# First attention values: a weight's cast ahead of the tile of h, its low parts behind the scaled tile, the next tile's modulation last

## The chip, the cores and the metric

One core of a Trainium2 chip runs the whole kernel in one launch. The metric is device time in microseconds; lower is better. Times are medians of several runs; the profile comes from one profiled execution, whose own time is given beside its span. The engines are TensorE (PE in the profile; PEld is its weight load), VectorE (DVE), ScalarE (ACT), GpSimd (POOL) and SyncE (SP), which issues nearly all transfers.

## The reference

One decoder block on x (1024 tokens by 1024 features) with a conditioning vector c. What matters here is its start:

```python
mod = silu(c) @ w_ada + b_ada
sh1, sc1, g1, sh2, sc2, g2 = split(mod, 6)
h = rms_norm(x, norm1_g) * (1 + sc1) + sh1
proj = h @ w_in        # retention q, k, v, gate; attention q, k, v for 3 groups of heads; 2 gates
```

Then come retention, dilated window attention in three groups, a gated merge with an output projection, a second normalised and modulated h with a squared-ReLU MLP, and a last RMS normalisation. Everything is float32.

## The kernel before, in words

**Number format.** TensorE multiplies fp32r operands. Each float32 operand is split into a high part (a cast to fp32r, on ScalarE) and a low part (the rest, a subtraction on VectorE). A product is the sum of three matmuls: low weight with high x, high weight with low x, high with high.

**Layout of the start.** h is kept transposed, as 8 tiles of 128 features by 1024 tokens: `hh[k]` high, `hl[k]` low. The normalisation's row factor is one row `rb1`, copied to all 128 partitions. The shift and the scale of tile k are columns `SH1 + k` and `SC1 + k` of `mods`, each the row sums of a 128x1024 tile of `w_ada` (`early`, shown as `em`) times a tile that holds silu(c) in every partition (`cb`). One such product with its sum is one VectorE instruction and a read of the accumulator.

**What is done for one tile** (helpers at lines 428 to 462):

- `mod1(k, parts)` (L433): the two products with row sums for scale and shift, from `early` tiles that SyncE loads in the start.
- `h1_mods(k)` (L448, L449): two instructions on 128x1 columns: add the bias to the shift, make the factor `a1`.
- `h1_scale(k)` (L456, L458): VectorE scales the tile `xt[k]` by `a1` and `rb1`, then ScalarE adds the shift and casts: `hh[k]`.
- `h1_low(k)` (L461): VectorE: `xt[k]` + shift - `hh[k]`, the low part `hl[k]`. It needs `hh[k]`.

**First attention values** (`av_first`, L768; `av_k`, L735). The values of attention group g are h @ w_av[g], 8 blocks of 128 tokens by 512 columns, one PSUM bank each, all 8 banks in use. For each k there are 24 matmuls of 128x512: from k = 1 on first 16 with `hh[k]` (low and high weight in turn), then 8 with `hl[k]`. For group 0 the tiles of h are made while they are used: the body of step k makes the tile k + 1 and the modulation of k + 2, and then issues the matmuls of k. One weight tile of 128x1024 covers two k's, so `ahead(1)` in every even k prepares the next step's weight. The start-up (`startup`, L371) has prepared the first weight, tile 0 of h and the modulation of tile 1.

**Weights.** `split_w` (L180) does both parts at once: the cast on ScalarE (L183), the subtraction on VectorE (L184). `split_first` (L759) does the cast alone (L762) and puts the subtraction (L763) on the list `first["lows"]`, to be called later; before, only the very first weight uses it.

**What sets the order.** There is no scheduler: each engine runs its instructions in the order in which the program emits them, and waits on semaphores for the others. `Steps` (L55) walks through a list of steps with their loads; three raw weight buffers (`raw`) are in turn, and the weight parts have three buffers each. `prepare` casts a loaded tile and then issues the load that takes the next buffer in turn; that transfer, on SyncE's queue (L85), waits until the old contents are read, which is after the subtraction. `first["release"]()` at k = 3 lets the loads beyond the first three be issued; SyncE itself runs ahead as far as its waits let it. The order of SyncE's queue in the stage is: the `em` and `xt` tiles with three weights between, four more weights, the attention bias tables (`bias_out`, L421), the next weight, the stores of the values.

**Behind it** the attention values of groups 1 and 2 follow (`av_step`, L832), then queries, keys and gates.

Of the kernel before, what the change touches and what calls it, by code (L numbers as in the profile page):

```python
# [20 lines left out]
NK = D // P  # L21
# [111 lines left out]
def block_kernel(ctx, tc, io, stop=None, dbg=None):  # L133
# [3 lines left out]
    def fv(t):  # L137
        return t.bitcast(F32)
# [36 lines left out]
    SH1, SC1, G1, SH2, SC2, G2 = (8 * i for i in range(6))  # L175

    steps = Steps(nc, wraw, 3)
# [187 lines left out]
    first = {"lows": []}  # L365
# [55 lines left out]
    def bias_out(g):  # L421

        nc.sync.dma_start(brow_d[g], bias_cut(rows, g)[:12])
        for a in range(4):
            src = brow_d[g][4 * g + a:4 * g + a + 1]
            nc.sync.dma_start(bias_d[g][a], src.to_broadcast([P, 384]))

    def mod1(k, parts=(SC1, SH1)):

        for i in parts:  # L430
            i += k
            t = early[i]
            nc.vector.scalar_tensor_tensor(t, t, 1.0, cb, op0=ALU.mult, op1=ALU.mult, accum_out=mods[:, i:i + 1])  # L433
# [12 lines left out]
    def h1_mods(k):  # L446
        sh = mods[:, SH1 + k:SH1 + k + 1]
        nc.vector.tensor_add(sh, sh, vec[:, VC_BADA + SH1 + k:VC_BADA + SH1 + k + 1])  # L448
        nc.vector.scalar_tensor_tensor(a1[:, k:k + 1], mods[:, SC1 + k:SC1 + k + 1], bs1[:, k:k + 1],  # L449
                                       vec[:, VC_N1 + k:VC_N1 + k + 1], op0=ALU.add, op1=ALU.mult)  # L450

    def h1_scale(k, j=None):

        ts = slice(0, S) if j is None else slice(512 * j, 512 * j + 512)
        t = xt[k][:, ts]
        nc.vector.scalar_tensor_tensor(t, t, a1[:, k:k + 1], rb1 if j is None else first["rb"][j],  # L456
                                       op0=ALU.mult, op1=ALU.mult)
        nc.scalar.activation(hh[k][:, ts], t, AF.Identity, bias=mods[:, SH1 + k:SH1 + k + 1])  # L458

    def h1_low(k):  # L460
        nc.vector.scalar_tensor_tensor(hl[k], xt[k], mods[:, SH1 + k:SH1 + k + 1], fv(hh[k]),  # L461
                                       op0=ALU.add, op1=ALU.subtract)
# [263 lines left out]
    def wsplit(ap):  # L726
        return ap, split_w
# [7 lines left out]
    def av_k(g, k, w):  # L735

        ws = slice((k % 2) * 512, (k % 2) * 512 + 512)
        if k == 0:
            av[g] = [ps_s(f"av{g}{c}") for c in range(NC)]
        if g == 0:  # L740

            parts = ((hh, 0), (hl, 0), (hh, 1)) if k == 0 else ((hh, 1), (hh, 0), (hl, 0))
            groups = (parts[:1], parts[1:2], parts[2:]) if k == 0 else (parts[:2], parts[2:])
        else:
            parts = ((hh, 1), (hh, 0), (hl, 0))
            groups = (parts,)
        for group in groups:
            for c in range(NC):
                for x, j in group:
                    nc.tensor.matmul(av[g][c], x[k][:, c * C:(c + 1) * C], w[j][:, ws], start=k == 0 and (x, j) == parts[0],  # L750
                                     stop=k == NK - 1 and (x, j) == parts[2], skip_group_check=True)
        for c in range(NC) if k == NK - 1 else ():
            if c % 2 == 0:
                t = x4(f"avo{g}{c}")
            o = t[:, DV * (c % 2):DV * (c % 2) + DV]
            nc.scalar.copy(o, av[g][c])
            nc.sync.dma_start(va_d[g][c * C:(c + 1) * C], o)
# [10 lines left out]
    def av_first(kk):  # L768

        def body(ahead, w):  # L770
            for k in (2 * kk, 2 * kk + 1):
                if k == 0:
                    for j, rb in enumerate(first["rb"]):
                        nc.scalar.copy(rb1[:, 512 * j:512 * j + 512], rb)
                if k + 1 < NK:
                    h1_mods(k + 1)
                    h1_scale(k + 1)
                    if k % 2 == 0:
                        ahead(1)
                    if k + 2 < NK:  # L780
                        mod1(k + 2)
                    h1_low(k + 1)
                av_k(0, k, w)
                if k == 3:
                    first["release"]()
                if k == 4:
                    for g in range(3):
                        bias_out(g)
                if k == NK - 1:
                    ahead(1)  # L790
                    nc.sync.dma_start(cs, io["cossin"])
                    nc.sync.dma_start(decay, io["decay"])
        return body
# [8 lines left out]
    def sums_of_h(name):  # L802

        low = None
        for m in range(4):
            k = 2 * m + 1
            e, o = xt[2 * m], xt[k]
            e0, e1, o0, o1 = e[:, :512], e[:, 512:], o[:, :512], o[:, 512:]
            sh = mods[:, SH1 + k:SH1 + k + 1]
            if name == "t1":  # L810
                r = e0
                nc.vector.tensor_sub(r, e0, e1)
            elif name == "t3":
                r = e1
                nc.vector.scalar_tensor_tensor(r, e1, dsh1[:, m:m + 1], o1, op0=ALU.add, op1=ALU.subtract)
            elif name == "t2":
                r = o1
                nc.vector.scalar_tensor_tensor(r, o1, sh, e0, op0=ALU.add, op1=ALU.add)
            else:
                r = o0  # L820
                nc.vector.scalar_tensor_tensor(r, o0, sh, o1, op0=ALU.add, op1=ALU.subtract)
            if name != "t4":
                t = x4(f"xa{name}{m}", F32R)
                XA[name, m] = t[:, :512], t[:, 512:]
            if low:
                nc.vector.tensor_sub(low[0], low[1], fv(low[2]))
            hi, lo = XA[name, m]
            nc.scalar.copy(hi, r)
            low = lo, r, hi
        nc.vector.tensor_sub(low[0], low[1], fv(low[2]))  # L830

    def av_step(g, kk):  # L832
        def body(w):
            if (g, kk) == (1, 0):
                for m in range(4):
                    nc.sync.dma_start(h12_d[m][:, 0], fv(hh[2 * m][:, 512:]))
                    nc.sync.dma_start(h12_d[m][:, 1], fv(hl[2 * m][:, 512:]))
                sh = mods[:, SH1:SH1 + NK].rearrange("p (m j) -> p m j", j=2)
                nc.vector.tensor_sub(dsh1, sh[:, :, 0], sh[:, :, 1])
            for k in (2 * kk, 2 * kk + 1):  # L840
                av_k(g, k, w)
            if g == 1 and kk < 3:
                sums_of_h(("t1", "t3", "t2")[kk])
            if (g, kk) == (1, 3):
                a_load(0, 1)
                a_load(0, 2)
            if (g, kk) == (2, 1):
                BA.prep((0, "11"), (0, "s1"))
            if (g, kk) == (2, 2):
                a_load(1, 1)  # L850
                a_load(1, 2)
                BA.prep((0, "s3"), (0, "s2"))
        return body
# [9 lines left out]
    def a_load(q, part):  # L863
        pair = PAIRS[q]
        src = io[{"g": "w_gate2", "a": "w_aq"}.get(pair[0]) or f"w_r{pair[1]}"]
        i = 2 * pair[1] + pair[2] if pair[0] == "a" else pair[-1]
        if q == 0 or q % 2 == 0 and part == 2:
            r = x4(f"wa{q}{part}")
        else:
            r = wraw.tile([P, 1024], F32, tag="raw", name=f"wa{q}{part}")  # L870
        nc.sync.dma_start(r, src[2 * i + part - 1])
        BA.raw[q, part] = r
# [67 lines left out]
        new_head(0)  # L940

    for kk in range(4):
        steps.add(av_first(kk), [(io["w_av"][kk], split_w if kk else split_first)], manual=True)
    for g in (1, 2):
        for kk in range(4):
            steps.add(av_step(g, kk), [wsplit(io["w_av"][4 * g + kk])])
    steps.mark()
    steps.add(queries_keys, manual=True)

# [3 lines left out]
    for h in range(H):  # L953
        steps.add(v_first(h), [wsplit(io["w_rv"][4 * h + j]) for j in range(2)], manual=True)
        steps.add(v_rest(h), [(io["w_rv"][4 * h + j], wv_prep) for j in range(2, 4)], manual=True)
        for c in range(NC):
            steps.add((lambda h, c: lambda ahead, *w: chunk(h, c, ahead, *w))(h, c),
                      ([wsplit(io["w_rg"][4 * h + c // 2])] if c % 2 == 0 else []) + [mod_load(later_mods[8 * h + c])],
                      manual=True)
# [418 lines left out]
    for pair in range(2):  # L1378
        for i, (g, a) in enumerate(combos):
# [3 lines left out]
                      manual=i == pair == 0)  # L1383
# [591 lines left out]
```

## Time and profile before

| | |
|---|---|
| median of 3 runs | 2317.35 us (2315.91 to 2317.53) |
| profiled execution, its own time | 2316.94 us |
| its span, first to last instruction | 2315.0 us |
| mean granted TensorE clock | 0.998 |
| ScalarE casts of weights in the stage | at 20.76, 31.67, 45.06, 58.46 and 71.85 us |
| first attention values: first matmul, first matmul of the next group | 23.37 us, 78.00 us |

How to read the rows. In a timeline: start in us from the span's start, duration in us, engine, source line, operation, output <- inputs with partitions x elements and type, count; in brackets the idle time before it and what ended it. In the table by stretches: start and end, length, then for each engine the busy time and the number of instructions, the granted clock of TensorE (1.00 is full), the busy share of the 16 transfer engines and GB/s. In the list of waits: who waited for whom, us in total, times, longest. An instruction's duration includes the end of its pipeline; the next one on the engine can start up to 0.1 us before that, so distances between starts are the better measure.

### The profile page before, as it was taken

Reading aid. Unit: us, or ns where it says so; the run is one execution under the profiler, and the core shown is the slowest. Engines: PE = TensorE matmul, PEld = TensorE weight load, DVE = VectorE, ACT = ScalarE, POOL = GpSimd, SP = SyncE. Lnnn points to the kernel's source line nnn. Section 1 sums busy time; section 2 is a strip of 40 time slices with the busy share of each in tenths; the row PEclk is TensorE's granted clock in tenths of the full one; section 3 lists DMA queues with packets and bytes.
Section 4 is the critical chain, followed back from the end, with each engine's and each line's share of the span. In section 5 each row is a group of like instructions: output and inputs, shape, how many; then the busy total and the mean of one; then the engine's idle time right before and its main releaser. Section 6 shows DMA issues by size and latency. Waiting matters only on the chain.

```text
span 2315.0 us, 26666 instructions
## 1 busy us (share of the span) xinstructions
PE 2261.9 (98%) x10466; PEld 1864.6 (81%) x10466; DVE 1350.1 (58%) x1986; ACT 808.2 (35%) x1479; POOL 171.7 (7%) x136
## 2 busy tenths in 40 slices
PE   6999999999999999999999999999999999999998
PEld 4787888888878787888788888888778887888887
DVE  5626555547677676855555646567855554544445
ACT  3324233222334343444535411134454444221112
POOL 0000000001101010100000014401000000000003
PEclk9999999999999999999999999999999999999999
DMA  8532333332323232233323353253223336323222
GB/s 350 192 127 99 115 114 110 110 133 104 118 86 126 89 119 91 83 130 102 96 72 96 136 174 97 90 189 118 68 108 109 109 108 218 111 91 103 98 82 73
DMA packets 101661, 274.65 MB, mean 119 GB/s; under 512 B 22423, under 2 KB 33950, under 8 KB 101407
## 3 DMA queue, kind: packets, MB, share of 16 engines
q1 hardware_dynamic: 100382, 270.85, 34.1%
q0 software_dynamic: 1152, 2.10, 0.3%
q8 instruction: 82, 1.34, 0.2%
q14 instruction: 45, 0.36, 0.1%
HBM read 208.27 MB, written 67.00 MB: 119 GB/s over the span
## 4 chain that ended last, share of the span: by engine, by line
PE 57%; DVE 5%; ACT 3%; DMA 1%; issue 1%; POOLq 0%; SPq 0%; POOL 0%; DVEq 0%; ACTq 0%
PE f L193 4%; PE f L197 4%; PE f L195 4%; PE fp L193 4%; PE fp L197 4%; PE fp L195 4%; PE ro L195 3%; PE ro L193 3%; PE ro L197 3%; PE ak L193 2%; PE ak L195 2%; PE ak L197 2%; PE rg L195 1%; PE rg L193 1%; PE wo L193 1%; PE wo L195 1%
## 5 line engine op out<-in xcount | busy, mean ns | idle before, releaser
L1768 DVE SCALAR_TENSOR_TENSOR x1r<-f,mods,x1r 128x512 f32<-128x512 f32 x112 | 78.7, 746 | 153.4 <-PE f L197 153.4
L1479 POOL TENSOR_TENSOR g<-g,rt 128x1024 f32<-128x1024 f32 x24 | 66.2, 2760 | 432.2 <-DVE rt L1478 432.2
L193 PE MATMUL qap<-hh,qaw 128*128 128x512 f32 x216 | 84.3, 390 | 3.4 <-DVE qat L277 1.7
L197 PE MATMUL qap<-hh,qaw 128*128 128x512 f32 x216 | 84.1, 389 | 0.0
L195 PE MATMUL qap<-hl,qaw 128*128 128x512 f32 x216 | 84.0, 389 | 0.0
L1478 DVE TENSOR_TENSOR rt<-ro,g 128x1024 f32<-128x1024 f32 x32 | 39.0, 1219 | 57.4 <-PE ro L197 45.2
L555 POOL TENSOR_TENSOR j<-qk,j 128x512 fp32r<-128x512 f32 x32 | 44.0, 1374 | 364.0 <-ACT j L554 364.0
L1619 ACT ACTIVATE a<-a 128x512 f32<-128x512 f32 x48 | 30.4, 633 | 110.1 <-DVE a L1618 110.1
L1521 POOL TENSOR_TENSOR accnf<-accnf,sqnf 128x256 f32<-128x256 f32 (+1 forms) x18 | 16.6, 924 | 654.5 <-ACT sqnf L1520 654.5
L250 DVE TENSOR_TENSOR qaw<-wa,qaw 128x512 fp32r<-128x512 f32 x54 | 36.7, 689 | 39.5 <-ACT qaw L240 39.5
L1109 ACT ACTIVATE P<-P,ng 128x128 f32<-128x128 f32 (+1 forms) x96 | 41.9, 438 | 40.1 <-DVE ng L1106 40.1
L250 DVE TENSOR_TENSOR fw<-w1r,fw 128x512 fp32r<-128x512 f32 x48 | 32.8, 688 | 36.2 <-ACT fw L240 36.2
L193 PE MATMUL fp<-h2h,fw 128*128 128x512 f32 x128 | 50.6, 395 | 0.5 <-ACT ft2nsq L272 0.5
L193 PEld LDWEIGHTS qap<-hh,qaw 128*128 128x128 f32 x216 | 40.5, 188 | 12.6 <-DVE qat L277 2.2
L197 PE MATMUL fp<-h2h,fw 128*128 128x512 f32 x128 | 50.3, 393 | 0.0
L195 PE MATMUL fp<-h2l,fw 128*128 128x512 f32 x128 | 50.2, 392 | 0.0
L633 ACT CAST vh<-v 128x512 fp32r<-128x512 f32 x32 | 18.8, 588 | 89.3 <-PE v L597 87.2
L575 ACT COPY sm<-sT 128x128 f32<-128x128 f32 x32 | 8.5, 267 | 113.9 <-PE sT L566 113.9
L197 PEld LDWEIGHTS qap<-hh,qaw 128*128 128x128 f32 x216 | 40.5, 188 | 8.5
L195 PEld LDWEIGHTS qap<-hl,qaw 128*128 128x128 f32 x216 | 40.5, 188 | 8.3
L240 ACT CAST qaw<-wa 128x512 fp32r<-128x512 f32 x54 | 32.5, 616 | 36.1 <-PE qap L197 36.1
L438 DVE SCALAR_TENSOR_TENSOR raw<-raw,cb 128x1024 f32<-128x1024 f32 x32 | 43.3, 1354 | 0.0
(3521 smaller groups left out, 6943.5 us busy)
## 6 DMA issues: line engine op xcount, KB each, us to landing
raw<-in_w_ada_dram SPq DMA_DIRECT2D x32, 512.0 KB, 3.5
w1r<-in_w_ff_dram SPq DMA_DIRECT2D x32, 512.0 KB, 5.2
ad<-a SPq DMA_DIRECT2D x32, 512.0 KB, 3.0
raw<-in_w_ff_dram SPq DMA_DIRECT2D x32, 512.0 KB, 3.5
raw<-ad SPq DMA_DIRECT2D x32, 512.0 KB, 4.4
em<-in_w_ada_dram SPq DMA_DIRECT2D x16, 512.0 KB, 10.2
qkd<-qa SPq DMA_DIRECT2D x16, 512.0 KB, 2.6
raw<-in_w_rv_dram SPq DMA_DIRECT2D x16, 512.0 KB, 4.4
```

The lines of the kernel that those rows point to most:

```text
L193: nc.tensor.matmul(o, wl, xh, start=first, stop=False, skip_group_check=skip)
L195: nc.tensor.matmul(o, wh, xl, start=False, stop=False, skip_group_check=skip)
L197: nc.tensor.matmul(o, wh, xh, start=False, stop=last, skip_group_check=skip)
L240: nc.scalar.copy(t[:, :512], src)
L250: nc.vector.tensor_sub(t[:, 512:], src, fv(t[:, :512]))
L438: nc.vector.scalar_tensor_tensor(raw, raw, 1.0, cb, op0=ALU.mult, op1=ALU.mult, accum_out=mods[:, i:i + 1])
L555: nc.gpsimd.tensor_sub(t[:, 1], src, fv(t[:, 0]))
L1109: nc.scalar.activation(v, v, AF.Exp, bias=ng[:, blk:blk + 1], accum_out=st[:, g, blk, 2 + a:3 + a])
L1478: nc.vector.tensor_mul(t, flat(ps), sg)
L1479: (nc.vector if h == H - 1 else nc.gpsimd).tensor_add(m, m, t)
L1619: nc.scalar.activation(o, o, AF.Relu)
L1768: nc.vector.scalar_tensor_tensor(x, ps[hf], mods[:, G2 + i:G2 + i + 1], x, op0=ALU.mult, op1=ALU.add)
```

## The change

In `av_first` three things move, and the kind of preparation of four weights changes.

- `ahead(1)`, which casts the next weight, stands at the top of an even k, in front of the tile k + 1. ScalarE thus does the cast ahead of that tile's activation.
- All weights that this stage prepares (those of steps 1 to 3 of group 0 and of step 0 of group 1) now go through `split_first`. Their subtraction is called behind the scaling of the tile k + 1, in front of its low parts.
- `h1_low(k + 1)` comes ahead of `mod1(k + 2)` where a weight was subtracted (even k), and between the scale's and the shift's part where not (odd k). Before, it came behind both.

The order of one tile's instructions on VectorE:

| | before | after |
|---|---|---|
| even k | mods, scaling, weight low, modulation x2, h low | mods, scaling, weight low, h low, modulation x2 |
| odd k | mods, scaling, modulation x2, h low | mods, scaling, modulation, h low, modulation |

and on ScalarE for an even k: before the activation, then the cast; after the cast, then the activation. The counts of instructions on all engines stay the same, and so does the order on TensorE and SyncE. For the last subtraction of the stage there is a call behind the matmuls of k = 7, which finds an empty list.

```diff
@@ -772,14 +772,23 @@
                     for j, rb in enumerate(first["rb"]):
                         nc.scalar.copy(rb1[:, 512 * j:512 * j + 512], rb)
+                if k % 2 == 0:
+                    ahead(1)
                 if k + 1 < NK:
                     h1_mods(k + 1)
                     h1_scale(k + 1)
-                    if k % 2 == 0:
-                        ahead(1)
-                    if k + 2 < NK:
-                        mod1(k + 2)
-                    h1_low(k + 1)
+
+                    if first["lows"]:
+                        first["lows"].pop(0)()
+                        h1_low(k + 1)
+                        if k + 2 < NK:
+                            mod1(k + 2)
+                    elif k + 2 < NK:
+                        mod1(k + 2, (SC1,))
+                        h1_low(k + 1)
+                        mod1(k + 2, (SH1,))
+                    else:
+                        h1_low(k + 1)
                 av_k(0, k, w)
@@
                 if k == NK - 1:
                     ahead(1)
+                    if first["lows"]:
+                        first["lows"].pop(0)()
@@
     for kk in range(4):
-        steps.add(av_first(kk), [(io["w_av"][kk], split_w if kk else split_first)], manual=True)
+        steps.add(av_first(kk), [(io["w_av"][kk], split_first)], manual=True)
     for g in (1, 2):
         for kk in range(4):
-            steps.add(av_step(g, kk), [wsplit(io["w_av"][4 * g + kk])])
+            steps.add(av_step(g, kk), [(io["w_av"][4 * g + kk], split_first if (g, kk) == (1, 0) else split_w)])
```

## The prediction

> **What bounds the kernel now.** I read the page first, then a table by stretches, then the waits, then the timelines of VectorE, ScalarE and TensorE for the first attention group.
>
> ```profile
> span 2315.0 us, 26666 instructions
> PE 2261.9 (98%) x10466; PEld 1864.6 (81%) x10466; DVE 1350.1 (58%) x1986; ACT 808.2 (35%) x1479; POOL 171.7 (7%) x136
> ```
>
> TensorE is busy 98% of the span, so an edit on another engine shows only where TensorE waits. The change sits in the first group's eight tiles of h, so I cut the time there at TensorE's starts of k = 1, 2, 4 and 6, its end, and the stage behind.
>
> ```profile
> core 0: us, PE busy (x) PEld busy (x) DVE busy (x) ACT busy (x) POOL busy (x), PEclk, DMA share, GB/s
> 31.82:40.20 8.38, 6.07 (x24) 4.35 (x24) 7.43 (x12) 2.03 (x2) 0.00 (x0) 1.00 1.03 410
> 40.20:53.59 13.39, 11.48 (x48) 8.85 (x48) 11.16 (x18) 3.24 (x3) 0.00 (x0) 1.00 0.96 382
> 53.59:66.99 13.40, 11.47 (x48) 8.86 (x49) 11.17 (x18) 3.24 (x3) 0.00 (x0) 1.00 0.18 55
> 66.99:78.00 11.01, 11.01 (x48) 9.12 (x49) 6.16 (x8) 3.48 (x5) 0.00 (x0) 1.00 0.49 131
> 78.00:158.00 80.00, 80.00 (x354) 66.25 (x353) 29.06 (x40) 24.20 (x37) 0.00 (x0) 1.00 0.47 164
> ```
>
> The same 48 matmuls take 11.01 us where nothing holds them (k = 6 and 7) and 13.39 us in the pairs before. In those, VectorE is busy 11.16 of 13.39 us. From 78.00 on TensorE has no gap for 80 us. So time won ahead of 78.00 is kept, as far as work shifts with it. Who waits for whom between 29 and 76 us:
>
> ```profile
> ACT hh L458 <- DVE xt L456: 35.1, 7, 6.3
> PE av L750 <- DVE hl L461: 4.4, 3, 1.7
> PE av L750 <- ACT hh L458: 3.0, 4, 1.2
> DVE raw_512l L184 <- ACT raw_512h L183: 2.2, 1, 2.2
> DVE raw_282l L184 <- ACT raw_282h L183: 2.2, 1, 2.2
> ```
>
> TensorE waits for the two halves of a tile of h (hh from ScalarE, hl from VectorE); ScalarE waits for VectorE's scaled tile (xt). VectorE's own wait is for the cast of a weight (4 of 2.2 us; first and last shown). So the chain is VectorE's list per tile, plus this wait in every second one.
>
> **The change, part by part.** VectorE's rows for one pair of tiles, k = 1 (odd) and k = 2 (even), then ScalarE's for the even one:
>
> ```profile
> 37.68 1.28 DVE L456 SCALAR_TENSOR_TENSOR xt<-xt,a,rb 128x1024 f32<-128x1024 f32 x1
> 38.88 1.22 DVE L433 SCALAR_TENSOR_TENSOR em<-em,cb 128x1024 f32<-128x1024 f32 x1
> 40.03 1.22 DVE L433 SCALAR_TENSOR_TENSOR em<-em,cb 128x1024 f32<-128x1024 f32 x1
> 41.17 1.28 DVE L461 SCALAR_TENSOR_TENSOR hl<-xt,mods,hh 128x1024 fp32r<-128x1024 f32 x1
> 42.37 0.15 DVE L448 TENSOR_TENSOR mods<-mods,vec 128x1 f32<-128x1 f32 x1
> 42.69 1.29 DVE L456 SCALAR_TENSOR_TENSOR xt<-xt,a,rb 128x1024 f32<-128x1024 f32 x1
> 46.13 1.23 DVE L184 TENSOR_TENSOR raw_294l<-raw,raw_294h 128x1024 fp32r<-128x1024 f32 x1 [2.16 <-ACT raw_294h L183]
> 47.27 1.22 DVE L433 SCALAR_TENSOR_TENSOR em<-em,cb 128x1024 f32<-128x1024 f32 x1
> 51.07 1.28 DVE L456 SCALAR_TENSOR_TENSOR xt<-xt,a,rb 128x1024 f32<-128x1024 f32 x1
> ...
> 44.01 1.15 ACT L458 ACTIVATE hh<-xt,mods 128x1024 fp32r<-128x1024 f32 x1 [3.86 <-DVE xt L456]
> 45.06 1.03 ACT L183 CAST raw_294h<-raw 128x1024 fp32r<-128x1024 f32 x1
> ```
>
> From start to start, one scaling takes 1.20 us (37.68 to 38.88), half a modulation 1.15, low parts of h 1.20 (41.17 to 42.37), the small operations 0.32 (42.37 to 42.69), low parts of a weight 1.14 (46.13 to 47.27). From one scaling to the next is 5.01 us for the odd tile and 8.38 for the even one.
>
> *The cast ahead (removes).* In the even tile VectorE is free at 42.69 + 1.20 = 43.89 and starts the weight's low parts at 46.13: 2.24 us in which ScalarE does first the activation, then the cast. In the changed order on ScalarE the cast stands in front of the activation, with nothing new between, so it can run while ScalarE idles (3.86 us before the activation). The low parts then follow the scaling at once.
>
> *Low parts of h ahead of the modulation (adds a wait).* With the scaling at S, the activation starts at S + 1.32 (44.01 - 42.69), ends 1.15 later at S + 2.47, and VectorE goes on 0.04 after that (46.13 against the cast's end at 45.06 + 1.03 = 46.09): low parts of h at S + 2.51 at the earliest. In the even tile the weight's low parts fill S + 1.20 to S + 2.34, in the odd one half the modulation fills S + 1.20 to S + 2.35, so 0.17 or 0.16 us of waiting is left. Behind it in VectorE's queue stand the next modulation, the small operations and the next scaling, so all of TensorE's supply pays it.
>
> *Modulation last (adds a wait).* The small operations read what the modulation just accumulated. Now the low parts of h lie between; in the new order they follow at once. The trace has this once, in the start:
>
> ```profile
> 28.81 0.08 DVE L433 DVE_READ_ACCUMULATOR em<-em,cb 128x1 f32 x1
> 28.92 0.16 DVE L448 TENSOR_TENSOR mods<-mods,vec 128x1 f32<-128x1 f32 x1
> 29.00 0.21 DVE L449 SCALAR_TENSOR_TENSOR a<-mods,bs,vec 128x1 f32<-128x1 f32 x1
> 29.30 1.28 DVE L456 SCALAR_TENSOR_TENSOR xt<-xt,a,rb 128x1024 f32<-128x1024 f32 x1
> ```
>
> The small operation starts 0.11 us after the accumulator's read, where behind low parts of h there is no such gap. I take 0.11 per tile; the same rows give 0.38 for the small operations instead of 0.32, so the other end is 0.17, and the low end is nothing.
>
> By the Trainium skill ("VectorE: DVE Perf Modes", section "The DRAIN you can't avoid") a semaphore between chained VectorE operations costs nothing extra. That speaks for 0 instead of 0.11 per tile; the row at 28.92 speaks against it, though it is one case, and the result by that rule is a rival below.
>
> *Sum.* New even tile: 2.51 + 1.20 + 2.29 (two halves) + 0.11 + 0.32 = 6.43 (8.38 before). New odd tile: 2.51 + 1.20 + 1.15 + 0.11 + 0.32 = 5.29 (5.01 before). A pair takes 11.72 instead of 13.39. The start up to the scaling at 29.30 keeps its order. That is an even tile, so the next scaling comes at 35.73 instead of 37.68 (1.95 won), and two pairs later, for the tile of k = 6, at 35.73 + 2 x 11.72 = 59.17 instead of 64.47.
>
> ```profile
> 40.20 0.50 PE L750 MATMUL av<-raw_282l,hh 128*128 128x512 f32 x1 [0.59 <-ACT hh L458]
> 66.99 0.50 PE L750 MATMUL av<-raw_510l,hh 128*128 128x512 f32 x1 [0.59 <-ACT hh L458]
> 64.47 1.28 DVE L456 SCALAR_TENSOR_TENSOR xt<-xt,a,rb 128x1024 f32<-128x1024 f32 x1
> ```
>
> TensorE starts k = 2 and k = 6 2.52 us behind their scalings (40.20 - 37.68; 66.99 - 64.47). New: k = 2 at 38.25, k = 4 at 49.97, k = 6 at 61.69. Its own work of 11.01 us per pair ends at 49.26 and 60.98, 0.71 us ahead of the tile it needs, so VectorE remains the limit, narrowly. After k = 6 nothing holds it: the end is at 61.69 + 11.01 = 72.70 instead of 78.00. **Won: 5.30 us.** The waits for hl go, since low parts of h now come before half or all of the modulation; the stall in the last even tile wins nothing, because TensorE has its own work there.
>
> *Transfers.* The cast carries the issue of a later weight's transfer with it, and stands ahead of an activation; is its weight there? And is the modulation's data there earlier?
>
> ```profile
> 15.63 0.33 SPq L85 DMA_DIRECT2D raw<-in_w_av_dram  x1
> 16.91 0.33 SPq L332 DMA_DIRECT2D em<-in_w_ada_dram  x1
> 24.60 0.33 SPq L85 DMA_DIRECT2D raw<-in_w_av_dram  x1
> 37.44 1.61 SPq L332 DMA_DIRECT2D em<-in_w_ada_dram  x2
> 41.29 0.33 SPq L85 DMA_DIRECT2D raw<-in_w_av_dram  x1
> raw<-in_w_av_dram SPq DMA_DIRECT2D x1, 512.0 KB, 10.6
> 60.77 0.33 SPq L85 DMA_DIRECT2D raw<-in_w_av_dram  x1
> ```
>
> At 10.6 us to landing (the row of the issue at 41.29) the first two casts' weights land at 26.2 and 35.2, with their activations due at 30.62 and 42.34. The third is the tight one: issued at 41.29, landed at 51.9; its activation is due at 52.74 + 1.32 = 54.06, so the 1.03 us cast must start by 53.0: 1.1 us of slack, by which I cost it at nothing. The modulations need data that landed at 27.5 (first shown) and 48.0 (last tile) at 33.0 and 60.4. SP's order stays the same; the transfer at 60.77 waits for the third weight's low parts and so leaves at about 55; the bias tables behind it come earlier too, and nobody in this stage waits for either.
>
> By the Trainium skill ("DMA: Bandwidth & Descriptors", section "Queues, rings and completion order") completion is not first in, first out, so the transfer issued behind the third weight, which now leaves some 4 us sooner, could hold it up. From this case: even a whole transfer more in front (512 KB at 410 GB/s, 1.28 us) leaves 51.9 + 1.3 = 53.2, and takes 0.2 us from the sum.
>
> The profiled execution took 2316.94 us, so the sum gives 2316.94 - 5.30 = **2311.6 us**. The median of the three runs is 0.4 above the profiled one (2317.35), the lowest 1.0 below it; the profiled one is near their mean, so I keep 2311.6.
>
> **The rivals.**
>
> 1. *The wait on the accumulator is free.* Five tiles up to k = 6 are each 0.11 shorter: 5.85 us won, 2311.1. For it: the gap of 0.11 is seen once only, in the start. Against: that one row. It is the time that the rule of the Trainium skill's page on VectorE, named above, would give.
> 2. *The chain costs more per tile.* At 0.17 per tile and the third cast 0.2 late, 4.8 are won; if every handover between the engines costs 0.2 more in the new order, where each tile has one, 5 x 0.2 go as well, which leaves about 3.8: 2313.1. For it: VectorE now waits for ScalarE in every tile, not in every second. Against: the handovers seen take 0.04.
> 3. *The gain doesn't reach the end.* Work behind 78.00 is paced by something that doesn't shift: 2316.9. The transfers of the start do not shift, but they are in by 53 (DMA share 0.18 in the third stretch), and the row of 80.00 busy us says TensorE paces itself. The same time would come out if the stall returned whole as the low parts' wait for the activation; the rows give 0.17 for it.
> 4. *Slower: the cast blocks the activation.* ScalarE's queue is in order. If the third weight lands after 53.0, each us delays that activation, the tile's low parts and all behind by one us; before, the cast stood behind the activation. From a landing at 58.3 the change loses (53.0 + 5.30), from 62.9 by over 0.2%; at 65 the time is 2323.6. For it: the queue moves 410 GB/s without a pause and that weight is among its last. Against: 10.6 us to landing, in a stream that doesn't change.
>
> **How the numbers follow.** Forecast 0.68, rival 1 0.10, rival 2 0.12, rival 3 0.06, rival 4 0.04. A measurement of this kernel tells about 0.2% from no change, 4.6 us: under 2312.7 counts as faster. The forecast is 1.1 us below that line and the runs differ by 1.6, so I give it 0.92 on the faster side; with rival 1 (0.99) and a little of rival 2 (0.05): faster 0.73, slower 0.04, the rest 0.23. The range goes from rival 1 on a low run (2315.91 is 1.0 below the profiled one: 2311.1 - 0.7) to rival 2 with 0.7 for a high one: 2310.4 to 2313.8. It leaves out rivals 3 and 4 and tails, under 0.2.
>
> **What would show it.** VectorE's 2.2 us waits for casts gone, and a wait of about 0.2 for hh before each hl in their place; scalings 6.4 and 5.3 apart; 0.1 between the accumulator's read and the small operation; all casts ahead of their activations with no wait for a transfer at the third; TensorE at k = 2, 4, 6 at 38.2, 50.0, 61.7 and at the next group at 72.7, without a gap from there. I am wrong if scalings are further apart, if the third activation waits behind its cast, or if the stage ends 5 us earlier and the span doesn't.

## The result, and the profile after

The changed kernel takes 2311.9 us (median of 14 runs, 2310.31 to 2313.15), the kernel before, run beside it, 2317.05 us (14 runs, 2315.21 to 2318.27). The ratio is 0.9978, 95% interval 0.9971 to 0.9986: faster by 5.1 us, 0.22%. The profiled execution of the changed kernel took 2311.34 us with a span of 2309.5 us, 5.5 us less than the span before.

Who waits for whom in the changed kernel, 29 to 74 us (us in total, times, longest; three of the five rows):

```profile
ACT hh L458 <- DVE xt L456: 27.3, 7, 5.3
PE av L750 <- ACT hh L458: 3.0, 4, 1.2
ACT raw_510h L762 <- DMA raw<-in_w_av_dram: 1.7, 1, 1.7
```

VectorE's four waits of 2.2 us for a cast are gone, and so are TensorE's 4.4 us for hl. New is ScalarE's wait of 1.7 us for the weight of the third cast. ScalarE's rows for the second and the third cast, each with the activation behind it:

```profile
38.27 1.04 ACT L762 CAST raw_294h<-raw 128x1024 fp32r<-128x1024 f32 x1
42.51 1.16 ACT L458 ACTIVATE hh<-xt,mods 128x1024 fp32r<-128x1024 f32 x1 [3.19 <-DVE xt L456]
51.85 1.05 ACT L762 CAST raw_510h<-raw 128x1024 fp32r<-128x1024 f32 x1 [1.74 <-DMA raw<-in_w_av_dram]
54.25 1.15 ACT L458 ACTIVATE hh<-xt,mods 128x1024 fp32r<-128x1024 f32 x1 [1.35 <-DVE xt L456]
```

The casts now stand in ScalarE's idle time. Even behind the third one, 1.35 us are left before the activation; the prediction saw 1.1 us of slack there.

VectorE's order in the bodies of k = 1 (odd) and k = 2 (even) in the changed kernel. As in the prediction, a tile is called odd or even by the k whose body makes it; the tile of k = 6 is made in the body of k = 5.

```profile
35.45 0.08 DVE L433 DVE_READ_ACCUMULATOR em<-em,cb 128x1 f32 x1
35.57 0.16 DVE L448 TENSOR_TENSOR mods<-mods,vec 128x1 f32<-128x1 f32 x1
35.90 1.29 DVE L456 SCALAR_TENSOR_TENSOR xt<-xt,a,rb 128x1024 f32<-128x1024 f32 x1
37.10 1.22 DVE L433 SCALAR_TENSOR_TENSOR em<-em,cb 128x1024 f32<-128x1024 f32 x1
38.24 0.08 DVE L433 DVE_READ_ACCUMULATOR em<-em,cb 128x1 f32 x1
38.40 1.28 DVE L461 SCALAR_TENSOR_TENSOR hl<-xt,mods,hh 128x1024 fp32r<-128x1024 f32 x1
41.19 1.28 DVE L456 SCALAR_TENSOR_TENSOR xt<-xt,a,rb 128x1024 f32<-128x1024 f32 x1
42.39 1.22 DVE L763 TENSOR_TENSOR raw_294l<-raw,raw_294h 128x1024 fp32r<-128x1024 f32 x1
43.70 1.28 DVE L461 SCALAR_TENSOR_TENSOR hl<-xt,mods,hh 128x1024 fp32r<-128x1024 f32 x1
47.64 1.28 DVE L456 SCALAR_TENSOR_TENSOR xt<-xt,a,rb 128x1024 f32<-128x1024 f32 x1
```

Scalings are 5.29 us apart for the odd tile (35.90 to 41.19) and 6.45 for the even one (41.19 to 47.64); forecast were 5.29 and 6.43. The small operation starts 0.12 us behind the accumulator's read (35.45 to 35.57), and low parts of h wait for the activation: they start at 38.40 where the read before them started at 38.24 (without a wait both start together, as at 41.17 in the kernel before), and 1.31 us behind the weight's low parts (42.39 to 43.70), which take 1.14 when nothing waits.

TensorE in the changed kernel, first matmuls of k = 2, 4 and 6 (in brackets the idle time before), then of the next group, and the table by stretches for the 80 us from there:

```profile
38.42 0.50 PE L750 MATMUL av<-raw_282l,hh 128*128 128x512 f32 x1 [0.70 <-ACT hh L458]
50.16 0.50 PE L750 MATMUL av<-raw_294l,hh 128*128 128x512 f32 x1 [0.57 <-ACT hh L458]
61.90 0.50 PE L750 MATMUL av<-raw_510l,hh 128*128 128x512 f32 x1 [0.57 <-ACT hh L458]
72.92 0.39 PE L750 MATMUL av<-raw_512l,hh 128*128 128x512 f32 x1
```

```profile
72.92:152.92 80.00, 80.00 (x354) 66.25 (x353) 29.08 (x40) 24.18 (x37) 0.00 (x0) 1.00 0.46 164
```

Forecast were 38.25, 49.97, 61.69 and 72.70. The start of this execution is 0.16 us later (first matmul of the stage at 23.53 instead of 23.37), the rest agrees within 0.06. From 72.92 on TensorE has again no gap for 80 us, and the medians of the whole time differ by 5.1 us: the gain is kept.

### The profile page after: what moved, and what is told of

The parts are those of the page before. It is cut to its first block, busy times and chain, and to the rows that moved or that the text cites. A ratio compares the mean times of both kernels' runs of the same rounds, so it can differ in the third digit from the quotient of the medians.

```text
span 2309.5 us, 26666 instructions
## 1 busy us (share of the span) xinstructions
PE 2259.8 (98%) x10466; PEld 1863.7 (81%) x10466; DVE 1351.4 (59%) x1986; ACT 808.1 (35%) x1479; POOL 171.6 (7%) x136
## 4 chain that ended last, share of the span: by engine, by line
PE 86%; DVE 7%; ACT 3%; issue 1%; DMA 1%; SPq 0%; DVEq 0%; POOLq 0%; POOL 0%; ACTq 0%
PE qap L193 5%; PE qap L197 5%; PE qap L195 5%; PE f L197 4%; PE f L195 4%; PE f L193 4%; PE av L750 4%; PE fp L193 4%; PE fp L197 4%; PE fp L195 3%; PE rg L193 3%; PE rg L195 3%; PE ro L195 3%; PE ro L193 3%; PE ro L197 3%; PE rg L197 3%
```

## Experiments

For all of them I measure the stage as the time from its first matmul to the first of the next group, so that the offset of the start drops out; before it is 78.00 - 23.37 = 54.63 us.

| kernel | stage, us | against before | ratio of whole times, 95% interval |
|---|---|---|---|
| changed | 49.39 | -5.24 | 0.9978 (0.9971 to 0.9986) |
| cast alone | 48.67 | -5.96 | 0.9970 (0.9958 to 0.9981) |
| cast alone, again | 48.68 | -5.95 | 0.9975 (0.9966 to 0.9985) |
| cast alone, third weight earlier | 47.95 | -6.68 | 0.9973 (0.9964 to 0.9983) |
| modulation last alone | 57.21 | +2.58 | 1.0011 (1.0001 to 1.0020) |
| the same, two gaps filled | 56.14 | +1.51 | 0.9999 (0.9990 to 1.0008) |
| whole split ahead of the tile | 50.37 | -4.26 | 0.9982 (0.9973 to 0.9991) |
| low parts of weights on GpSimd | 52.87 | -1.76 | 0.9990 (0.9981 to 0.9999) |
| changed, third weight late | 51.48 | -3.15 | 0.9987 (0.9978 to 0.9997) |
| before, third weight late | 54.65 | +0.02 | 0.9999 (0.9990 to 1.0008) |

0.0010 of the time is 2.3 us, so an interval of a ratio is about 4 us wide: it tells the large differences apart, the stage's length in the trace (one execution each) the small ones. The granted clock adds to the scatter of whole times: between the stage and the kernel's last 10 us the traces have no (changed kernel), one (before) or two (cast alone, modulation last alone) further stretches of 3.41 us at a clock of 0.50, each worth up to 1.7 us (an estimate: half its length).

**Cast alone.** The changed kernel with the modulation back ahead of the low parts of h:

```diff
                     if first["lows"]:
                         first["lows"].pop(0)()
-                        h1_low(k + 1)
-                        if k + 2 < NK:
-                            mod1(k + 2)
-                    elif k + 2 < NK:
-                        mod1(k + 2, (SC1,))
-                        h1_low(k + 1)
-                        mod1(k + 2, (SH1,))
-                    else:
-                        h1_low(k + 1)
+                    if k + 2 < NK:
+                        mod1(k + 2)
+                    h1_low(k + 1)
```

> The changed kernel with the modulation put back ahead of the low parts of h; the cast stays ahead and the weight's low parts stay behind the scaling. Theory (the whole gain comes from the cast, and modulation last costs 0.28 us per tile: 0.16 of waiting for the activation and 0.12 for the accumulator): scalings 6.15 and 5.01 us apart (1.20 + 1.14 + 2.29 + 1.20 + 0.32, and the 5.01 of before) instead of 6.45 and 5.29; TensorE starts k = 2, 4, 6 at 38.0, 49.1, 60.3 and the next group at 71.3; 6.7 us faster than before, 1.5 faster than the changed kernel. Low parts of h come 5.95 us after the scaling and are needed 6.28 after it. The third weight lands at 51.9, its cast ends at 52.9, just when the activation is due. Rival (the low parts of h are what TensorE waits for, so they have to come first): waits of TensorE for hl come back, and the time is that of the changed kernel or more, 5.2 us faster than before or less.

Scalings of the cast alone (VectorE's timeline), the one wait left on VectorE, and the third cast on ScalarE:

```profile
40.56 1.28 DVE L456 SCALAR_TENSOR_TENSOR xt<-xt,a,rb 128x1024 f32<-128x1024 f32 x1
46.70 1.28 DVE L456 SCALAR_TENSOR_TENSOR xt<-xt,a,rb 128x1024 f32<-128x1024 f32 x1
51.71 1.28 DVE L456 SCALAR_TENSOR_TENSOR xt<-xt,a,rb 128x1024 f32<-128x1024 f32 x1
53.65 1.23 DVE L763 TENSOR_TENSOR raw_510l<-raw,raw_510h 128x1024 fp32r<-128x1024 f32 x1 [0.65 <-ACT raw_510h L762]
58.60 1.28 DVE L456 SCALAR_TENSOR_TENSOR xt<-xt,a,rb 128x1024 f32<-128x1024 f32 x1
...
52.56 1.06 ACT L762 CAST raw_510h<-raw 128x1024 fp32r<-128x1024 f32 x1 [3.38 <-DMA raw<-in_w_av_dram]
```

An even tile takes 6.14 us (40.56 to 46.70), an odd one 5.01. For hl only one of TensorE's weight loads waits, 0.2 us (the rival said more). The stage is 0.72 us shorter than in the changed kernel, so moving the modulation costs and brings nothing. It would be about 1.4 shorter, and the 6.7 expected would be reached, but for the third weight: landed at 52.56, it holds VectorE at 53.65, and the even tile made in the body of k = 4 takes 6.89 (51.71 to 58.60). The next experiment takes this wait away.

**Third weight earlier.** Run beside a second run of the cast alone:

```diff
+        first["issue"] = issue
-        for k in range(NK):
+        for k in range(NK - 1):
             early_load(k)
...
                 av_k(0, k, w)
+                if k == 1:
+                    first["issue"](4)
+                    early_load(NK - 1)
```

> The cast alone, with the transfer of the third weight put in front of the last tile's three transfers, so that it leaves 3.8 us sooner (3 x 1.28). Theory (what is left of VectorE's waiting in the kernel with the cast alone, 0.65 us at 53.65, is this weight's landing): the third cast runs by 50, scalings 6.15 and 5.01 apart throughout, TensorE's k = 6 at 60.4 instead of 61.1, 0.7 us faster than the cast alone. Rival (the last tile's data come too late then, or the landing was not what held it): no faster than the cast alone.

> The cast alone once more, beside the next kernel: 7 us faster than before, the third cast waiting for its weight, TensorE's k = 6 at 61.1.

The third cast in the cast alone, again, and with the third weight earlier (its lines are shifted by 1):

```profile
52.47 1.05 ACT L762 CAST raw_510h<-raw 128x1024 fp32r<-128x1024 f32 x1 [3.41 <-DMA raw<-in_w_av_dram]
...
49.10 1.03 ACT L763 CAST raw_439h<-raw 128x1024 fp32r<-128x1024 f32 x1
```

The repeated cast alone is as it was: the third cast waits, TensorE's k = 6 starts at 61.02, and 5.95 us are won in the stage, 6.0 in the medians, not 7. With the third weight earlier that cast runs at 49.10 without a wait, all even tiles take 6.13 to 6.14, and TensorE goes from k = 3 to 4 and from 5 to 6 without idle time. The stage is 0.73 us shorter than in the cast alone beside it (48.68 to 47.95), as the theory has it. In the whole time that doesn't show: medians 2310.71 and 2310.83 us, 2316.86 before.

**Modulation last alone.** The same order of modulation in the kernel before, with the cast behind the activation as it was:

```diff
                     if k % 2 == 0:
                         ahead(1)
-                    if k + 2 < NK:
-                        mod1(k + 2)
-                    h1_low(k + 1)
+                        h1_low(k + 1)
+                        if k + 2 < NK:
+                            mod1(k + 2)
+                    elif k + 2 < NK:
+                        mod1(k + 2, (SC1,))
+                        h1_low(k + 1)
+                        mod1(k + 2, (SH1,))
+                    else:
+                        h1_low(k + 1)
```

> The kernel before with only the modulation moved behind the low parts of h; the cast stays behind the activation. Theory (cast makes the gain): scalings 8.49 and 5.29 us apart instead of 8.38 and 5.01, the one of k = 6 0.9 us later, so 0.9 us slower than before, although TensorE's waits for hl (4.4 us in three) all go. Rival (TensorE's waits for hl are part of what bounds the stage): up to 4 us faster.

TensorE's waits for hl all go, and the kernel is slower (2319.27 us beside 2317.59): they bound nothing. But the stage is 2.58 us longer, not 0.9. VectorE's part is as expected:

```profile
28.76 1.28 DVE L456 SCALAR_TENSOR_TENSOR xt<-xt,a,rb 128x1024 f32<-128x1024 f32 x1
64.87 1.28 DVE L456 SCALAR_TENSOR_TENSOR xt<-xt,a,rb 128x1024 f32<-128x1024 f32 x1
```

From the first scaling (28.76) to that of k = 6 (64.87) it takes 36.11 us, against 35.17 before (29.30 to 64.47), 0.94 more. The rest is TensorE's clock. The granted clock is the last but two of the columns:

```profile
38.00:39.79 1.79, 0.00 (x0) 0.00 (x0) 1.72 (x4) 1.15 (x1) 0.00 (x0) 1.00 1.02 405
39.79:41.00 1.21, 1.21 (x5) 1.03 (x6) 1.21 (x2) 0.00 (x0) 0.00 (x0) 0.95 1.04 413
42.00:43.00 1.00, 1.00 (x4) 0.75 (x3) 0.93 (x5) 0.00 (x0) 0.00 (x0) 0.50 1.01 401
45.00:46.00 1.00, 1.00 (x6) 0.84 (x5) 0.00 (x0) 0.97 (x2) 0.00 (x0) 1.00 1.02 406
```

TensorE was idle for 2.78 us ahead of 39.79; the first matmuls then run at 1.00, the clock falls to 0.50, and by 45 it is back. At 0.50 the matmuls start 0.43 us apart (42.05, 42.48, 42.91), at 1.00 0.23 (40.13, 40.36, 40.59). Ahead of k = 6 it is the same:

```profile
67.39 0.50 PE L750 MATMUL av<-raw_510l,hh 128*128 128x512 f32 x1 [2.62 <-ACT hh L458]
68.61 0.63 PE L750 MATMUL av<-raw_510l,hh 128*128 128x512 f32 x1
72.76 2.00 PE L750 MATMUL av<-raw_510h,hl 128*128 128x512 f32 x8
```

The first 16 matmuls of k = 6 take 5.37 us (67.39 to 72.76) where they take 3.76 at full clock (40.20 to 43.96 in the kernel before): 1.61 lost, and 0.94 + 1.61 = 2.55 of the 2.58. The first drop costs nothing at the end, because TensorE waits for VectorE again behind it.

**Two gaps filled.** Is it the gap that lowers the clock? Modulation last alone, with matmuls by a tile of zeros in those two gaps (`zero` is set once in the start):

```diff
                 av_k(0, k, w)
+                if k in (1, 5):
+                    for c in range(NC):
+                        nc.tensor.matmul(av[0][c], hh[k][:, c * C:(c + 1) * C], zero,
+                                         start=False, stop=False, skip_group_check=True)
```

> Modulation last alone, with 8 more matmuls with a tile of zeros behind k = 1 and behind k = 5, in the two gaps of 2.8 and 2.6 us after which TensorE's granted clock fell to 0.50. They take 1.8 us each and add nothing to the result. Theory (the gaps lower the clock): gaps shorten to about 1 us, the granted clock stays at 1.00, the 16 matmuls behind take 3.8 us instead of 5.4, and the kernel gets about 1 us slower than before instead of 2.5. Rival (the clock falls for another reason, or the slow matmuls are not what cost the time): the clock falls again, or the time is that of modulation last alone.

```profile
39.80:44.00 4.20, 3.96 (x17) 3.30 (x18) 4.05 (x8) 0.19 (x1) 0.00 (x0) 1.00 1.04 413
...
55.00:58.00 3.00, 3.00 (x10) 2.32 (x9) 2.83 (x6) 0.07 (x1) 0.00 (x0) 0.55 0.00 0
```

```profile
53.84 0.50 PE L752 MATMUL av<-raw_296l,hh 128*128 128x512 f32 x1 [2.65 <-ACT hh L460]
```

These are, in the table by stretches, the one behind the first filled gap and one behind the start of k = 4, and then, in TensorE's timeline, that start. Behind both filled gaps the clock stays at 1.00. The gap ahead of k = 4, which was 1.02 us long as long as k = 2 ran slowly, is now 2.65 us, and the drop has moved there. So the drop follows TensorE's idle time and not a place in the program. The stage is 1.07 us shorter than without the filling; the 1.51 left against before are the 0.94 of VectorE and 0.6 by which the late k = 5 and the filling push k = 6. In the whole time (no difference from before that can be measured) the interval is too wide to tell 1 us from 0.

**Whole split ahead of the tile.** The shortest edit of all: in the kernel before, `ahead(1)` goes to the top of the even k with both parts of the split.

```diff
+                if k % 2 == 0:
+                    ahead(1)
                 if k + 1 < NK:
                     h1_mods(k + 1)
                     h1_scale(k + 1)
-                    if k % 2 == 0:
-                        ahead(1)
```

> The kernel before with the whole preparation of the weight, cast and low parts, put ahead of the tile in even k; modulation as before. Theory: VectorE's work per pair is 11.16 us as with the cast alone, but the low parts of the weight now stand in front of the scaling, so VectorE waits for the third weight: it gets there at about 51.3, the cast of the weight that lands at 51.9 ends at 52.9, 1.6 us later. The tile of k = 1 comes 1.14 later as well. TensorE's k = 6 at 61.9, next group at 73.0, 5.0 us faster than before. Rival (transfers play no part): 6.4 us faster.

VectorE's and ScalarE's rows at the third weight:

```profile
52.96 1.23 DVE L184 TENSOR_TENSOR raw_510l<-raw,raw_510h 128x1024 fp32r<-128x1024 f32 x1 [1.84 <-ACT raw_510h L183]
54.42 1.28 DVE L456 SCALAR_TENSOR_TENSOR xt<-xt,a,rb 128x1024 f32<-128x1024 f32 x1
...
51.88 1.05 ACT L183 CAST raw_510h<-raw 128x1024 fp32r<-128x1024 f32 x1 [3.06 <-DMA raw<-in_w_av_dram]
```

VectorE waits 1.84 us for the cast (1.6 expected), now ahead of the scaling. 4.26 are won instead of 5.0. I had put the delayed tile only against k = 6; TensorE already waits for it at k = 5 (56.94) and reaches k = 6 at 62.51, 0.6 us later than its tile allows (59.42 + 2.52 = 61.94). Low parts of a weight behind the scaling are thus worth something: there the third weight costs 0.65 us.

**Low parts on GpSimd.** The cast alone, with the subtractions of the four later weights on GpSimd:

```diff
+    seen = []
+
     def split_first(raw):
...
-        first["lows"].append(lambda: nc.vector.tensor_sub(lo, raw, fv(hi)))
+        first["lows"].append(lambda e=nc.gpsimd if seen else nc.vector: e.tensor_sub(lo, raw, fv(hi)))
+        seen.append(1)
```

> The cast alone, with the low parts of four weights subtracted on GpSimd, which is idle in this stage. Theory: VectorE's list falls to 10.0 us per pair, below TensorE's 11.01, so TensorE is the limit from k = 1 on: k = 2 at 37.4, the end at 70.5, 7.5 us faster than before; the third activation waits for its cast until 52.9, which TensorE's lead covers. A subtraction takes some 2.7 us there (twice the 1.37 us of a 128x512 operation in the profile). Rival: GpSimd and VectorE hold each other up, VectorE's instructions get longer than 1.2 us, and less than 6.7 us are won.

VectorE's and GpSimd's rows around the first and the second of the four weights:

```profile
27.78 3.42 DVE L433 SCALAR_TENSOR_TENSOR em<-em,cb 128x1024 f32<-128x1024 f32 x1
38.98 1.22 DVE L433 SCALAR_TENSOR_TENSOR em<-em,cb 128x1024 f32<-128x1024 f32 x1
40.12 3.48 DVE L461 SCALAR_TENSOR_TENSOR hl<-xt,mods,hh 128x1024 fp32r<-128x1024 f32 x1
...
27.13 2.99 POOL L765 TENSOR_TENSOR raw_282l<-raw,raw_282h 128x1024 fp32r<-128x1024 f32 x1 [7.36 <-ACT raw_282h L764]
40.12 2.40 POOL L765 TENSOR_TENSOR raw_294l<-raw,raw_294h 128x1024 fp32r<-128x1024 f32 x1 [10.01 <-ACT raw_294h L764]
```

The rival holds: 1.76 us are won in the stage instead of 7.5. While GpSimd subtracts, one of VectorE's instructions takes 3.42 or 3.48 us instead of 1.22 or 1.28: 2.2 us lost to save 1.14. The Trainium skill ("SBUF — State Buffer", section "SBUF: two separate sides") has this as an exclusive lock for a whole instruction, not as a slowing of both; the 2.2 us agree with that, being nearly the 2.40 of GpSimd's instruction. The first such hold also leaves TensorE idle for 3.45 us ahead of k = 1 (30.70 to 34.15). Its clock falls to 0.50 already within that gap, at 32.82, and is back at 39.65.

**A late third weight.** In the changed kernel and in the one before, the rotation and decay tables are loaded ahead of that weight instead of at the end of the stage:

```diff
         for k in range(NK):
             early_load(k)
             if k in (0, 1, 3):
                 issue((k + 3) // 2)
+        nc.sync.dma_start(cs, io["cossin"])
+        nc.sync.dma_start(decay, io["decay"])
...
-                    nc.sync.dma_start(cs, io["cossin"])
-                    nc.sync.dma_start(decay, io["decay"])
```

> The changed kernel with the loads of the rotation table (1 MB) and the decay table (256 KB), which otherwise come at the end of the stage, put in front of the third weight's transfer, so that this weight lands 3.2 us later (1.25 MB at 410 GB/s), at about 55.1. Theory (the cast now blocks the activation when its weight lands after 53.0): the third cast ends at 56.1, that activation comes 2.0 us later than in the changed kernel, and so do the low parts, the scaling and TensorE's k = 6: 63.9, next group at 74.9, 3.2 us faster than before instead of 5.2. Rival (the transfer has more slack than the rows show, or the cast doesn't block): the time of the changed kernel, 5.2 us faster.

> The kernel before with the same two loads put in front of the third weight. Both theories: the cast stands behind the activation and starts at 58.5, 3 us after the weight lands, so nothing moves: within 0.5 us of before. If this one loses time too, it is the loads themselves and not the place of the cast.

ScalarE in the changed kernel with the late weight (its lines are shifted by 2), then TensorE's k = 6:

```profile
55.40 1.04 ACT L764 CAST raw_512h<-raw 128x1024 fp32r<-128x1024 f32 x1 [5.24 <-DMA raw<-in_w_av_dram]
56.35 1.14 ACT L460 ACTIVATE hh<-xt,mods 128x1024 fp32r<-128x1024 f32 x1
...
64.06 0.50 PE L752 MATMUL av<-raw_512l,hh 128*128 128x512 f32 x1 [0.77 <-ACT hh L460]
```

The weight lands at 55.40, the activation starts behind its cast at 56.35, and k = 6 at 64.06 (63.9 expected): 3.15 us won in the stage instead of 5.24. With the cast behind the activation the same loads change nothing (54.65 us, ratio 0.9999). So the cast does block, from about where the prediction put it, as far as one landing can tell: 55.40 less the 2.09 us lost is 53.3, or 53.1 without the 0.23 us by which this stage starts later than before (23.60 against 23.37); the prediction has 53.0.

## Why the prediction was right

- **What bounds the stage:** right. The wait of 2.24 us per even tile went, and TensorE's starts followed VectorE's scalings by 2.52 us as before (35.90 to 38.42, 47.64 to 50.16).
- **The sum:** 5.30 us forecast, 5.24 measured in the stage, 5.1 in the medians. The two waits that it adds were 0.16 or 0.17 for the activation (0.16 and 0.17 measured: 38.24 to 38.40, and 1.31 instead of 1.14) and 0.11 for the accumulator (0.12). That the median of 2311.9 us lies within 0.3 of the forecast is partly luck, since the runs lie 2.8 us apart; the rows of the stage are the better proof.
- **Rival 1** (the wait on the accumulator is free, 5.85 us) is out: the gap of 0.12 stands in all seven tiles. By the Trainium skill ("VectorE: DVE Perf Modes", section "The DRAIN you can't avoid") a semaphore between chained VectorE operations costs nothing extra, which would give 0 here; the measured 0.12 decides otherwise for the read of an accumulator and the operation that uses it. Whether the semaphore or something else in that dependence takes the time, no run shows.
- **Rival 2** (0.2 more per handover) is out: scalings are apart as forecast.
- **Rival 3:** the gain reaches the end; 80 us without a gap behind the stage.
- **Rival 4** did not occur, but its mechanism and price are right: with the weight 3.5 us later (51.85 to 55.40) the gain falls by 2.09 us. The slack was 1.35 us instead of 1.1: in the changed kernel the cast starts at 51.85 and ends at 52.90, the activation starts at 54.25. The sign "no wait for a transfer at the third" did not come out in these words, since ScalarE waited 1.74 us there, but in time that it had to spare. The transfer behind that weight left 3.1 us sooner (47.38 to 44.29) and did not hold it up (10.3 us to landing, 10.6 before).
- **Not seen by the prediction:** that it is worth nothing by itself when "the waits for hl go". They went, and in the cast alone TensorE meets hl within 0.2 us without moving any modulation. The moved modulation costs 1.4 us of the 6.7 that the cast wins (6.68 with the third weight earlier); the prediction priced it (0.28 per tile) without asking whether it is needed. And it took a gap of TensorE to cost its own length; in the changed kernel the longest gap in the stage is 1.20 us (1.72 before), so that did no harm.

The versions with the cast alone are ahead of the changed kernel in the stage (48.67 and, with the third weight earlier, 47.95 against 49.39 us). Their whole times, 2309.51 to 2310.83 us, were not measured beside the 2311.9, and the intervals of the ratios overlap, so the order of the whole times is not settled.

## What to carry to other kernels

When an engine stalls behind another engine's queue, look first at whether the work that it waits for could run in that queue's idle time, and at when its data land: a cast moved ahead inherits the wait for its transfer and gives it to everything behind. A wait that a profile lists is worth removing only if its end is the last to come; price each part of a change alone, since a part that removes three listed waits can still cost time. Keep gaps on TensorE short where they can't be removed.

## What the runs showed of the hardware that was not expected

- Less idle time on TensorE than was expected halved its granted clock. In this stage 0.50 followed gaps of 2.19 us (whole split ahead of the tile), 2.62 and 2.78 (modulation last alone), 2.65 (two gaps filled) and 3.45 (low parts on GpSimd), but not 1.72 (before) or 1.77 (before, third weight late). The length of a gap doesn't decide alone: later, one of 1.83 us (from 178.11, modulation last alone) was followed by 0.50 and one of 1.97 (from 174.44, low parts on GpSimd) was not.
- In the clock records of all eleven traces the changes lie a whole number of 3.41 us apart, whatever the work does. In modulation last alone half speed begins at 40.88, 68.19 and 180.83 us, 8 and 33 times 3.413 us apart. It lasted 3.41 us each time in this stage, twice that in low parts on GpSimd (32.82 to 39.65). It followed where TensorE was idle for 1.95 to 2.62 us of one such stretch; stretches at full speed with up to 1.60 us idle had no effect in this stage. Elsewhere it also followed a stretch with 0.91 us idle (from 1157.9, cast alone), so there is more to the rule, and that stays open. The Trainium skill ("TensorE: Matmul & The Clock Gate", section "What's actually happening") has a free-running window of about 3.4 us, and the records agree with that; by its table the clock falls after at least one idle window, and here a window idle in part was enough.
- One subtraction of 128x1024 on GpSimd takes 2.40 us where it starts together with a VectorE instruction (40.12), and 2.99 or 3.45 where such an instruction was already running (27.13, 53.95). Each time one of VectorE's instructions is held for 2.2 us.
- The landing of the third weight varies by up to 1 us between kernels that issue it at the same place: 10.3 us behind its issue in the changed kernel, 10.6 before, 11.0 in the cast alone, 11.3 with low parts on GpSimd. That the later weight's transfer leaves sooner doesn't explain it: it was issued at 44.29 in the changed kernel (10.3) and at 47.26 in modulation last alone (11.1). What decides stays open.
